# First pass of a two-layer transformer trunk: tables on other queues, one transfer per weight chunk, tokens in four parts, bias added behind the sums, one cast for both token blocks

## The chip, the cores and the metric

The kernel runs on 1 core of one Trainium2 chip. The metric is device time in microseconds. The kernel before took 645.62 us, the median of three runs (642.17 to 645.78).

The engines are named as the profile names them: PE does matmuls (PEld its weight loads), DVE is the vector engine, ACT the scalar engine, POOL the general one, SP issues most transfers.

## The reference

Two layers work on 256 tokens of width 1024. Layer 0 mixes tokens with block attention (one block of 256 here, so plain causal attention with 16 heads), layer 1 with differential attention; each is followed by a squared-ReLU MLP of width 4096. Each sub-layer's input is modulated by a vector c, and its output goes through a gate, a residual and a LayerNorm.

```
mod = jnp.einsum('bd,lde->lbe', jax.nn.silu(c), ada_w) + ada_b[:, None, :]
for i in range(DEPTH):
    shift1, scale1, gate1, shift2, scale2, gate2 = [m[:, None, :] for m in jnp.split(mod[i], 6, axis=-1)]
    h = x * (1.0 + scale1) + shift1
    y = moba_attention(h, ...)  # layer 0; layer 1: diff_attention(h, ...)
    x = layer_norm(DEEPNORM_ALPHA * x + (1.0 + gate1) * y, ln_g[i, 0], ln_b[i, 0])
    h = x * (1.0 + scale2) + shift2
    y = sq_relu_mlp(h, mlp_w_up[i], mlp_w_down[i])
    x = layer_norm(DEEPNORM_ALPHA * x + (1.0 + gate2) * y, ln_g[i, 1], ln_b[i, 1])
```

So before the first projection of layer 0 can start, silu(c), the two rows of `mod` for shift1 and scale1, and h must be there. `ada_w` reaches the kernel transposed, so that 128 outputs of `mod` are 128 partitions and the 1024 inputs lie along the row.

## The kernel before

All matmuls with weights are done in three products of rounded halves: a value is split into `hi` (a rounding cast on ACT) and `lo` (the difference, on DVE), and hi·hi + hi·lo + lo·hi are added in PSUM (`mm3`, lines L167 to L169). So each weight chunk that comes in as `raw` costs a cast on ACT (L130) and a subtraction on DVE (L131).

The **first pass** (`first_operand`, `first_products`) computes a first part of layer 0's q, k and v: columns 0 to 511 of each, for both token blocks of 128. It runs over the 8 chunks j of the contraction, 128 inputs each, and adds into six PSUM tiles (`kacc`: tags mm, sc, ac, for two blocks). For one chunk j it needs:

- two row sums for the modulation (`ada_rows`, L215 and L216): a 512 KB transfer of `ada_w` each into `aw`, then one DVE instruction that multiplies with silu(c) (`sbc`, spread over all partitions) and adds along the row, with the bias `ada_b` as the sum's start. They give the columns of `ab`, scale and shift; L499 adds 1 to the scale.
- the tokens: `xt` is transposed by PE into `tp` (L516), ACT forms `full` = tp·scale + shift (L518), then per block a cast to hi (L521) and a subtraction to lo (L522), both into `hT`.
- the weights: three transfers into one `raw` tile (L508 for v, L510 twice for q and k), then two casts and two subtractions, of 1024 and of 512 columns.
- 18 matmuls of 512 columns: 2 blocks, 3 outputs, 3 products.

The bias columns come from `tabT`, the transpose of a table `t1` (ada_b in 96 rows, ln_g in 32), which SP fetches ahead of the first `aw`; so does the identity `ident` that PE needs for all its transposes.

What is in which place on an engine is settled when the kernel is built: a scheduler orders each engine's instructions by its own estimate, and each engine then works through its list in order. Transfers are ordered the same way on the queue of the engine that issues them; SP's are tracked by eight semaphores in turn, so that an issue waits for the landing of the one eight places before. Buffers: `aw` tiles 2 and 3 (two tags), `raw` 3, `hi` and `lo` 8 each.

After the first pass the program string of layer 0 goes on with attention (V, Q, T, S, P, F steps), output projection, LayerNorm and MLP. Row sums for the other modulation vectors are done as fillers between.

Of the kernel before, what the change touches and what calls it, by code (L numbers as in the profile page):

```python
# [66 lines left out]
SHIFT1, SCALE1, GATE1, SHIFT2, SCALE2, GATE2 = range(6)  # L67
C_ID, C_ONE, C_MASK, C_ROPE = 0, 128, 256, 512
# [4 lines left out]
def tile_trunk(ctx: ExitStack, tc: tile.TileContext, x, c, moba_w_in, moba_w_out, diff_w_in, diff_w_out,  # L73
               lam_q1, lam_k1, lam_q2, lam_k2, subln_g, ada_wt, ada_b, ln_g, ln_b, w_up, w_down, cst, out):
    nc = tc.nc
    vec, act, pe, pool_e, sp = nc.vector, nc.scalar, nc.tensor, nc.gpsimd, nc.sync
# [5 lines left out]
    small = ctx.enter_context(tc.tile_pool(name="small", bufs=1))  # L82
# [10 lines left out]
    ident, ones = cs[:, C_ID:C_ID + P], cs[:, C_ONE:C_ONE + P]  # L93
    sbc = cpool.tile([P, D], F32, name="sbc")
    t1 = ap_.tile([P, P], F32, tag="nat", name="t1", bufs=3)
    t2 = ap_.tile([P, P], F32, tag="nat", name="t2", bufs=3)
    ccol = small.tile([P, 2, KC], F32, tag="ccol", name="ccol", bufs=1)
    sp.dma_start(out=ccol[:, 0, :], in_=c.rearrange("o (p k) -> p (o k)", k=KC))
    sp.dma_start(out=ident, in_=cst[:, C_ID:C_ID + P])
    sp.dma_start(out=t1[0:96, :], in_=ada_b.rearrange("l (j p) -> (l j) p", p=P))  # L100

    nhalf = small.tile([P, 1], F32, name="nhalf")
    pool_e.memset(nhalf, -0.5)

    act.activation(out=ccol[:, 1, :], in_=ccol[:, 0, :], func=AF.Exp, scale=-1.0)
    vec.tensor_scalar(out=ccol[:, 1, :], in0=ccol[:, 1, :], scalar1=1.0, scalar2=None, op0=ALU.add)
    vec.reciprocal(out=ccol[:, 1, :], in_=ccol[:, 1, :])
    vec.tensor_tensor(out=ccol[:, 1, :], in0=ccol[:, 1, :], in1=ccol[:, 0, :], op=ALU.mult)
# [15 lines left out]
        xt.append(xb)  # L124


    def split_piece(raw_ap, n=1024):
        hi = wp.tile([P, 1024], F32R, tag="hi", name="hi", bufs=8)
        lo = wp.tile([P, 1024], F32R, tag="lo", name="lo", bufs=8)
        act.copy(out=hi[:, :n], in_=raw_ap)  # L130
        vec.tensor_tensor(out=lo[:, :n], in0=raw_ap, in1=hi[:, :n], op=ALU.subtract)  # L131
        return hi, lo

    def raw_tile():
# [53 lines left out]
    cols = {}  # L188
    tabT = cpool.tile([P, P], F32, name="tabT")
    tabT2 = cpool.tile([P, P], F32, name="tabT2")  # L190

    def adab_cols(l, v):
        o = (l * 6 + v) * KC
        return tabT[:, o:o + KC]
# [13 lines left out]
            if filler:  # L208
                filler.popleft()()

    def ada_rows(l, v, j, dst, tag, bufs):

        aw = ap_.tile([P, D], F32, tag=tag, name="aw", bufs=bufs)
        r0 = v * D + j * P
        sp.dma_start(out=aw, in_=ada_wt[l, r0:r0 + P, :])  # L215
        vec.tensor_tensor_reduce(out=aw, in0=aw, in1=sbc, scale=1.0, scalar=adab_cols(l, v)[:, j:j + 1],  # L216
                                 op0=ALU.mult, op1=ALU.add, accum_out=dst)

    def queue_vector(l, v):
# [270 lines left out]
    hT0 = act_tiles()  # L490
# [3 lines left out]
    def first_operand(j):  # L494

        ab = small.tile([P, 2], F32, tag="ab0", name="ab0", bufs=3)
        ada_rows(0, SCALE1, j, ab[:, 0:1], "bc", 3)
        ada_rows(0, SHIFT1, j, ab[:, 1:2], "aw", 2)
        vec.tensor_scalar(out=ab[:, 0:1], in0=ab[:, 0:1], scalar1=1.0, scalar2=None, op0=ALU.add)  # L499
        def load_x(cols):  # L500
            for b in range(2):
                sp.dma_start(out=xt[b][:, cols], in_=x[0, b * P:(b + 1) * P, cols])

        if j == 0:
            load_x(slice(0, 256))
# [40 lines left out]
    tps = psum("tp")  # L546
# [16 lines left out]
    tps = psum("tp")  # L563
# [223 lines left out]
```

## Time and profile before

| | |
|---|---|
| median of three runs | 645.62 us |
| time of the profiled execution | 644.11 us |
| its span | 640.7 us |
| PE busy in the span | 609.0 us, 95% |
| DVE busy | 500.4 us, 78% |
| ACT busy | 377.6 us, 59% |
| POOL busy | 22.2 us, 3% |
| matmuls | 3140 |

The span is what the trace covers; 3.4 us of the execution's own time lie around it. An engine is busy when an instruction other than a wait or an issue runs on it. PE is busy for nearly the whole span except at its start and end, so a change in the first 55 us moves the end as far as it moves PE's work after them.

### The profile page before, as it was taken

The numbers are of one execution on the slowest core, as the hardware profiler recorded it, in microseconds if no ns is written. First come the engines' busy times: TensorE is split into PE (matmuls) and PEld (weight loads), VectorE is DVE, ScalarE is ACT, GpSimd is POOL, SyncE is SP. The second block draws the span as 40 slices with busy tenths as digits, with TensorE's granted clock in tenths as the row PEclk, the third lists the DMA queues.
The fourth block names the chain that finished last, engine by engine and source line by source line (L and its number), as shares of the span: only waits on it lengthen the run. The fifth ranks groups of instructions, "written<-read, shape, count | busy, mean of one in ns | idle before, by whom it ended". The sixth has DMA issues, their size and how long they took to land.

```text
span 640.7 us, 8768 instructions
## 1 busy us (share of the span) xinstructions
PE 609.0 (95%) x3140; PEld 499.6 (78%) x3140; DVE 500.4 (78%) x903; ACT 377.6 (59%) x699; POOL 22.2 (3%) x37
## 2 busy tenths in 40 slices
PE   4889999998999999999999999989999999999994
PEld 3667887886888888888877787767788888888883
DVE  5798998889978878888799989977984646465446
ACT  3448665657846545664477676765775556475530
POOL 0000000001000000000000010021100000000002
PEclk9999999999999999999999999999999999999998
DMA  8997998876689888989765967682663764746401
GB/s 292 406 322 279 313 325 286 288 250 227 215 309 343 308 313 330 326 294 338 268 231 188 337 229 263 232 289 68 208 218 109 259 225 143 255 133 213 182 0 66
DMA packets 65941, 158.23 MB, mean 247 GB/s; under 512 B 4041, under 2 KB 21098, under 8 KB 65898
## 3 DMA queue, kind: packets, MB, share of 16 engines
q1 hardware_dynamic: 65898, 157.68, 70.1%
q8 instruction: 24, 0.39, 0.2%
q14 instruction: 19, 0.16, 0.1%
HBM read 156.62 MB, written 1.05 MB: 246 GB/s over the span
## 4 chain that ended last, share of the span: by engine, by line
PE 64%; DVE 18%; DMA 6%; ACT 4%; issue 3%; POOL 2%; SPq 1%; DVEq 0%; POOLq 0%; ACTq 0%
PE ac L184 13%; PE sc L184 10%; PE mm L687 7%; PE tp L687 6%; DMA aw<-in_ada_w_dram 6%; DVE lo L131 5%; DVE aw L216 4%; PE mm L167 4%; PE mm L169 4%; PE mm L168 4%; PE mm L692 3%; PE tp L692 3%; ACT hi L130 2%; DVE z L292 1%; DVE z L289 1%
## 5 line engine op out<-in xcount | busy, mean ns | idle before, releaser
L131 DVE TENSOR_TENSOR lo<-raw,hi 128x1024 fp32r<-128x1024 f32 x196 | 232.0, 1197 | 44.1 <-ACT hi L130 40.4
L130 ACT CAST hi<-raw 128x1024 fp32r<-128x1024 f32 x196 | 201.3, 1034 | 62.5 <-PE sc L184 43.6
L216 DVE CUSTOM_DVE_ANT_0 aw<-aw,sbc,tabT 128x1024 f32<-128x1024 f32 x96 | 122.0, 1280 | 23.1 <-DMA aw<-in_ada_w_dram 22.7
L167 PE MATMUL mm<-hi,hT 128*128 128x512 f32 x224 | 90.6, 405 | 6.1 <-ACT hi L130 3.2
L169 PE MATMUL mm<-hi,hT 128*128 128x512 f32 x224 | 89.0, 398 | 0.0
L168 PE MATMUL mm<-lo,hT 128*128 128x512 f32 x224 | 88.6, 396 | 0.2 <-DVE lo L131 0.2
L687 PE MATMUL mm<-hT,hi 128*128 128x512 f32 x192 | 60.4, 396 | 0.0
L687 PE MATMUL tp<-hT,hi 128*128 128x512 f32 x192 | 60.3, 395 | 0.0
L167 PEld LDWEIGHTS mm<-hi,hT 128*128 128x128 f32 x224 | 42.3, 189 | 16.1 <-ACT hi L130 3.8
L184 PE MATMUL ac<-hi,sTh 128*128 128x512 f32 x160 | 51.2, 397 | 0.0
L184 PE MATMUL ac<-lo,sTh 128*128 128x512 f32 x160 | 50.8, 394 | 0.0
L184 PE MATMUL ac<-hi,sTl 128*128 128x512 f32 x160 | 50.4, 392 | 0.0
L169 PEld LDWEIGHTS mm<-hi,hT 128*128 128x128 f32 x224 | 42.3, 189 | 9.1 <-DVE hT L328 0.4
L168 PEld LDWEIGHTS mm<-lo,hT 128*128 128x128 f32 x224 | 42.3, 189 | 8.6 <-DVE lo L131 0.3
L184 PE MATMUL sc<-hi,sTh 128*128 128x512 f32 x144 | 45.3, 392 | 0.0
L184 PE MATMUL sc<-lo,sTh 128*128 128x512 f32 x144 | 45.1, 391 | 0.0
L184 PE MATMUL sc<-hi,sTl 128*128 128x512 f32 x144 | 44.6, 390 | 0.0
L692 PEld LDWEIGHTS tp<-hT,lo 128*128 128x128 f32 x192 | 34.4, 188 | 7.5
L692 PEld LDWEIGHTS mm<-hT,lo 128*128 128x128 f32 x192 | 34.4, 188 | 7.3
L697 ACT COPY nat<-mm 128x256 f32<-128x256 f32 x24 | 7.8, 376 | 52.4 <-PE mm L687 52.4
L692 PE MATMUL tp<-hT,lo 128*128 128x256 f32 x192 | 36.0, 279 | 0.0
L692 PE MATMUL mm<-hT,lo 128*128 128x256 f32 x192 | 35.9, 279 | 0.0
(153 smaller groups left out, 899.4 us busy)
## 6 DMA issues: line engine op xcount, KB each, us to landing
aw<-in_ada_w_dram SPq DMA_DIRECT2D x96, 512.0 KB, 5.5
raw<-in_mlp_w_up_dram SPq DMA_DIRECT2D x32, 1024.0 KB, 5.9
raw<-in_mlp_w_down_dram SPq DMA_DIRECT2D x32, 1024.0 KB, 5.1
raw<-in_diff_w_in_dram SPq DMA_DIRECT2D x16, 512.0 KB, 5.1
raw<-in_moba_w_in_dram SPq DMA_DIRECT2D x24, 256.0 KB, 5.5
raw<-in_moba_w_in_dram SPq DMA_DIRECT2D x8, 512.0 KB, 4.8
raw<-in_moba_w_out_dram SPq DMA_DIRECT2D x4, 1024.0 KB, 8.4
raw<-in_diff_w_in_dram SPq DMA_DIRECT2D x4, 1024.0 KB, 5.7
```

The source lines that it names most:

```text
L130: act.copy(out=hi[:, :n], in_=raw_ap)
L131: vec.tensor_tensor(out=lo[:, :n], in0=raw_ap, in1=hi[:, :n], op=ALU.subtract)
L167: pe.matmul(dst, lhsT=xh, rhs=wh, start=start, stop=False)
L168: pe.matmul(dst, lhsT=xh, rhs=wl, start=False, stop=False)
L169: pe.matmul(dst, lhsT=xl, rhs=wh, start=False, stop=stop)
L184: pe.matmul(dsts[h], lhsT=a, rhs=w[:, h * 512:(h + 1) * 512], start=start and k == 0 and i == 0, stop=stop and k == n - 1 and i == 2)
L216: vec.tensor_tensor_reduce(out=aw, in0=aw, in1=sbc, scale=1.0, scalar=adab_cols(l, v)[:, j:j + 1], op0=ALU.mult, op1=ALU.add, accum_out=dst)
L289: vec.tensor_tensor(out=z[:, c_], in0=accs[c_.start // 512][:, a0:a0 + c_.stop - c_.start], in1=gate[:, c_], op=ALU.mult)
L292: vec.scalar_tensor_tensor(out=z[:, c_], in0=xt[b][:, c_], scalar=ALPHA, in1=z[:, c_], op0=ALU.mult, op1=ALU.add)
L687: pe.matmul(ps, lhsT=w[k][0][:, c_], rhs=x3[k], start=first, stop=last)
L692: pe.matmul(ps[:, 0:S], lhsT=w[k][1][:, c_], rhs=x3[k][:, 0:S], start=False, stop=False)
L697: act.copy(out=r[:, i * S:(i + 1) * S], in_=ps[:, S:2 * S])
```

## The change

In words: `ident` is issued from ACT's queue, and the two parts of `t1` from POOL's, so SP issues the first `aw` right behind c. A chunk's weights come in one transfer of three pieces of 512 columns, q and k first in the tile, v last. The tokens come in four pairs of transfers of 256 columns (chunks 0, 2, 4, 6) in place of one pair of 256 columns and one of 768. The row sums start from 0; the biases (1 added to those of scale) lie in a new tile `tab1`, and one addition on two columns (L505 of the changed file) adds them behind the sums, shift first. `full` is cast to hi for both blocks by one ACT instruction and made into lo by one DVE instruction. Weight casts are written with v's 512 columns ahead of q's and k's 1024. `tabT` is copied by ACT in place of DVE. Three instructions (the exponential of c, the copy into `tab1`, the subtractions of chunk 0) are kept in the order of the program text.

```diff
-    sp.dma_start(out=ident, in_=cst[:, C_ID:C_ID + P])
-    sp.dma_start(out=t1[0:96, :], in_=ada_b.rearrange("l (j p) -> (l j) p", p=P))
+    act.dma_start(out=ident, in_=cst[:, C_ID:C_ID + P])
+    pool_e.dma_start(out=t1[0:96, :], in_=ada_b.rearrange("l (j p) -> (l j) p", p=P))
+    pool_e.dma_start(out=t1[96:128, :], in_=ln_g.rearrange("l i (j p) -> (l i j) p", p=P))
...
-    act.activation(out=ccol[:, 1, :], in_=ccol[:, 0, :], func=AF.Exp, scale=-1.0)
+    tc.keep_in_program_order(act.activation(out=ccol[:, 1, :], in_=ccol[:, 0, :], func=AF.Exp, scale=-1.0))
...
-    def ada_rows(l, v, j, dst, tag, bufs):
+    def ada_rows(l, v, j, dst, tag, bufs, bias=True):
...
-        vec.tensor_tensor_reduce(out=aw, in0=aw, in1=sbc, scale=1.0, scalar=adab_cols(l, v)[:, j:j + 1],
+        vec.tensor_tensor_reduce(out=aw, in0=aw, in1=sbc, scale=1.0, scalar=adab_cols(l, v)[:, j:j + 1] if bias else 0.0,
...
-        ada_rows(0, SCALE1, j, ab[:, 0:1], "bc", 3)
-        ada_rows(0, SHIFT1, j, ab[:, 1:2], "aw", 2)
-        vec.tensor_scalar(out=ab[:, 0:1], in0=ab[:, 0:1], scalar1=1.0, scalar2=None, op0=ALU.add)
+        ada_rows(0, SHIFT1, j, ab[:, 0:1], "bc", 3, False)
+        ada_rows(0, SCALE1, j, ab[:, 1:2], "aw", 2, False)
+        if j == 0:
+            tc.keep_in_program_order(vec.tensor_copy(out=tab1[:, 0:KC], in_=adab_cols(0, SHIFT1)))
+            vec.tensor_scalar(out=tab1[:, KC:], in0=adab_cols(0, SCALE1), scalar1=1.0, scalar2=None, op0=ALU.add)
+        vec.tensor_tensor(out=ab, in0=ab, in1=tab1[:, j:j + KC + 1:KC], op=ALU.add)
+        if j % 2 == 0:
             for b in range(2):
+                cols = slice(j * P, (j + 2) * P)
                 sp.dma_start(out=xt[b][:, cols], in_=x[0, b * P:(b + 1) * P, cols])
...
-        sp.dma_start(out=raw[:, 0:512], in_=wr[:, 2 * D:2 * D + 512])
-        for s_ in range(2):
-            sp.dma_start(out=raw[:, 512:1536].rearrange("p (g s n) -> p s g n", g=2, s=2)[:, s_],
-                         in_=wr[:, s_ * D:s_ * D + 512].rearrange("p (g n) -> p g n", n=256))
-        if j == 1:
-            load_x(slice(256, D))
+        sp.dma_start(out=raw[:, 0:1536].rearrange("p (s n) -> p s n", s=3),
+                     in_=wr.rearrange("p (s d) -> p s d", s=3)[:, :, 0:512])
...
-        act.activation(out=full[:, :256], in_=tp[:, :256], func=AF.Identity, scale=ab[:, 0:1], bias=ab[:, 1:2])
-        for b in range(2):
-            hi, lo = halves(hT0[j // 4], b)
-            act.copy(out=hi[:, j % 4, :], in_=full[:, b * P:(b + 1) * P])
-            vec.tensor_tensor(out=lo[:, j % 4, :], in0=full[:, b * P:(b + 1) * P], in1=hi[:, j % 4, :], op=ALU.subtract)
-        h1, l1 = split_piece(raw[:, 0:1024])
-        h2, l2 = split_piece(raw[:, 1024:1536], 512)
-        return [(h1[:, 0:512], l1[:, 0:512]), (h1[:, 512:1024], l1[:, 512:1024]), (h2[:, 0:512], l2[:, 0:512])]
+        act.activation(out=full[:, :256], in_=tp[:, :256], func=AF.Identity, scale=ab[:, 1:2], bias=ab[:, 0:1])
+        both = hT0[j // 4][:, j % 4, :]
+        act.copy(out=both[:, 0:2 * P], in_=full[:, :2 * P])
+        vec.tensor_tensor(out=both[:, 2 * P:], in0=full[:, :2 * P], in1=both[:, 0:2 * P], op=ALU.subtract)
+        v_w = [t[:, 0:512] for t in split_piece(raw[:, 1024:1536], 512, j == 0)]
+        qk_w = [t.rearrange("p (s n) -> p s n", s=2) for t in split_piece(raw[:, 0:1024], keep=j == 0)]
+        return [v_w] + [[t[:, :, g * 256:(g + 1) * 256] for t in qk_w] for g in range(2)]
...
-    vec.tensor_copy(out=tabT, in_=tps[:, 0:P])
+    act.copy(out=tabT, in_=tps[:, 0:P])
```

Since the scheduler orders the instructions anew, the change also moves work in the lists. On SP, the start of the program before; c is the conditioning vector, cs the constants with the identity, t the table, aw the rows of `ada_w`, raw the weights:

```order
L98 DMA ccol<-in_c_dram 128x8
L99 DMA cs<-in_constants_dram 128x128
L100 DMA t_73<-in_ada_b_dram 96x128
L533 DMA t_73<-in_ln_g_dram 32x128
L215 DMA aw<-in_ada_w_dram 128x1024 x2
L502 DMA x<-in_x_dram 128x256 x2
L508 DMA raw<-in_moba_w_in_dram 128x512
L510 DMA raw<-in_moba_w_in_dram 128x2x256 x2
```

and in the changed kernel:

```order
L98 DMA ccol<-in_c_dram 128x8
L218 DMA aw<-in_ada_w_dram 128x1024 x2
L509 DMA x<-in_x_dram 128x256 x2
L512 DMA raw<-in_moba_w_in_dram 128x3x512
```

Three issues ahead of the first `aw` are gone, and two of the three for `raw`.

On ACT, chunks 4 and 5 of the first pass before (raw_295 and full_302 belong to chunk 4, raw_342 and full_349 to chunk 5):

```order
L130 CAST hi_308<-raw_295 128x1024
L518 ACTIVATE full_302<-tp_299,ab0_287 128x256
L130 CAST hi_312<-raw_295 128x512
L521 CAST hT_102<-full_302 128x128 x2
L130 CAST hi_355<-raw_342 128x1024
L518 ACTIVATE full_349<-tp_346,ab0_334 128x256
L130 CAST hi_359<-raw_342 128x512
L521 CAST hT_102<-full_349 128x128 x2
```

and now (raw_284 and full_289 belong to chunk 4, raw_327 and full_332 to chunk 5):

```order
L518 ACTIVATE full_289<-tp_286,ab0_274 128x256
L520 CAST hT_103<-full_289 128x256
L131 CAST hi_293<-raw_284 128x512
L131 CAST hi_297<-raw_284 128x1024
L518 ACTIVATE full_332<-tp_329,ab0_319 128x256
L131 CAST hi_336<-raw_327 128x512
L520 CAST hT_103<-full_332 128x256
L131 CAST hi_340<-raw_327 128x1024
```

Before, the 1024-column cast of a chunk's weights stood ahead of that chunk's `full`; now both weight casts stand behind it. The chunks alternate between the two patterns shown: 2, 4 and 6 as chunk 4, and 3, 5 and 7 as chunk 5.

On DVE, chunk 4 before, from its row sums on:

```order
L216 ISA aw_288,ab0_287<-aw_288,sbc_72,tabT_99 128x1024
L216 ISA aw_291,ab0_287<-aw_291,sbc_72,tabT_99 128x1024
L499 TENSOR_SCALAR ab0_287<-ab0_287 128x1
L131 TENSOR_TENSOR lo_309<-raw_295,hi_308 128x1024
L131 TENSOR_TENSOR lo_313<-raw_295,hi_312 128x512
L522 TENSOR_TENSOR hT_102<-full_302,hT_102 128x128 x2
```

and now the end of chunk 3, chunk 4 and the start of chunk 5 (lo_253 belongs to chunk 3, ab0_319 to chunk 5):

```order
L219 ISA aw_275,ab0_274<-aw_275,sbc_72 128x1024
L132 TENSOR_TENSOR lo_253<-raw_239,hi_252 128x1024
L219 ISA aw_278,ab0_274<-aw_278,sbc_72 128x1024
L505 TENSOR_TENSOR ab0_274<-ab0_274,tab1_113 128x2
L521 TENSOR_TENSOR hT_103<-full_289,hT_103 128x256
L132 TENSOR_TENSOR lo_294<-raw_284,hi_293 128x512
L132 TENSOR_TENSOR lo_298<-raw_284,hi_297 128x1024
L219 ISA aw_320,ab0_319<-aw_320,sbc_72 128x1024
L219 ISA aw_323,ab0_319<-aw_323,sbc_72 128x1024
L505 TENSOR_TENSOR ab0_319<-ab0_319,tab1_113 128x2
```

In both, the subtractions stand behind the row sums and their addition; only in chunks 3, 5 and 7 does the first row sum of the next chunk now stand between the two subtractions. (Between two row sums the lists also hold the reading of the accumulator, left out here.)

## Rows read from the trace of the kernel before

**Rows 1.** Busy time in stretches (us, busy of each engine, clock, DMA share, GB/s).

```profile
12.00:30.00 18.00, 15.84 (x63) 12.18 (x64) 14.31 (x26) 7.29 (x16) 0.00 (x0) 1.00 1.05 402
30.00:50.00 20.00, 18.15 (x78) 13.57 (x76) 19.72 (x38) 10.28 (x21) 0.00 (x0) 1.00 0.93 340
55.00:100.00 45.00, 43.97 (x275) 35.23 (x273) 42.04 (x108) 32.76 (x77) 0.00 (x0) 1.00 0.85 289
100.00:160.00 60.00, 56.12 (x321) 45.42 (x321) 52.24 (x109) 36.12 (x79) 3.30 (x4) 1.00 0.76 260
```

**Rows 2.** Timeline of the start (start us, duration, engine, line, what, idle before and releaser).

```profile
0.72 1.28 ACT L105 ACT_TABLE_LOAD   x1 [0.72 <-PEq L771]
...
1.17 0.42 SPq L99 DMA_DIRECT2D cs<-in_constants_dram  x1
...
2.37 0.21 ACT L105 ACTIVATE ccol<-ccol 128x8 f32<-128x8 f32 x1 [0.37 <-DMA ccol<-in_c_dram]
2.57 0.90 SPq L215 DMA_DIRECT2D aw<-in_ada_w_dram  x2
2.61 0.17 DVE L106 TENSOR_SCALAR ccol<-ccol 128x8 f32<-128x8 f32 x1 [2.61 <-ACT ccol L105]
...
6.18 1.28 DVE L216 CUSTOM_DVE_ANT_0 aw<-aw,sbc,tabT 128x1024 f32<-128x1024 f32 x1 [0.24 <-DMA aw<-in_ada_w_dram]
...
8.76 0.15 DVE L499 TENSOR_SCALAR ab<-ab 128x1 f32<-128x1 f32 x1
...
10.70 1.56 ACT L130 CAST hi<-raw 128x1024 fp32r<-128x1024 f32 x2 [0.31 <-DMA raw<-in_moba_w_in_dram]
```

**Rows 3.** DMA issues of 0 to 60 us: KB each, median us to landing.

```profile
aw<-in_ada_w_dram SPq DMA_DIRECT2D x18, 512.0 KB, 8.0
...
cs<-in_constants_dram SPq DMA_DIRECT2D x1, 64.0 KB, 2.1
```

**Rows 4.** Timeline of ACT, chunk 3, and the first cast of chunk 4.

```profile
27.93 0.56 ACT L518 ACTIVATE full<-tp,ab 128x256 f32<-128x256 f32 x1 [3.91 <-DVE ab L499]
28.39 1.03 ACT L130 CAST hi<-raw 128x1024 fp32r<-128x1024 f32 x1
29.32 0.50 ACT L521 CAST hT<-full 128x128 fp32r<-128x128 f32 x2
29.72 0.62 ACT L130 CAST hi<-raw 128x512 fp32r<-128x512 f32 x1
31.00 1.05 ACT L130 CAST hi<-raw 128x1024 fp32r<-128x1024 f32 x1 [0.65 <-DMA raw<-in_moba_w_in_dram]
```

**Rows 5.** Timeline of DVE, chunk 3 to the end of chunk 4's row sums.

```profile
27.68 0.15 DVE L499 TENSOR_SCALAR ab<-ab 128x1 f32<-128x1 f32 x1
29.45 1.23 DVE L131 TENSOR_TENSOR lo<-raw,hi 128x1024 fp32r<-128x1024 f32 x1 [1.62 <-ACT hi L130]
30.60 0.49 DVE L522 TENSOR_TENSOR hT<-full,hT 128x128 fp32r<-128x128 f32 x2
31.00 0.68 DVE L131 TENSOR_TENSOR lo<-raw,hi 128x512 fp32r<-128x512 f32 x1
31.61 1.28 DVE L216 CUSTOM_DVE_ANT_0 aw<-aw,sbc,tabT 128x1024 f32<-128x1024 f32 x1
...
34.02 0.15 DVE L499 TENSOR_SCALAR ab<-ab 128x1 f32<-128x1 f32 x1
```

**Rows 6.** Timeline of DVE, the additions of chunks 6 and 7.

```profile
43.56 0.15 DVE L499 TENSOR_SCALAR ab<-ab 128x1 f32<-128x1 f32 x1
...
48.33 0.15 DVE L499 TENSOR_SCALAR ab<-ab 128x1 f32<-128x1 f32 x1
```

**Rows 7.** Timeline of PE: chunk 7's first and last matmul, and the next transposes.

```profile
49.90 0.50 PE L167 MATMUL mm<-hi,hT 128*128 128x512 f32 x1 [0.21 <-ACT hT L521]
...
53.90 0.39 PE L169 MATMUL ac<-hi,hT 128*128 128x512 f32 x1
...
55.59 0.63 PE L366 MATMUL tp<-cs,nat 128*128 128x128 f32 x4 [0.41 <-DVE nat L359]
```

More of the change, by code (lines that the diff above doesn't have):

```diff
@@ L124, in tile_trunk, with split_piece @@
         xt.append(xb)
-    def split_piece(raw_ap, n=1024):
+    def split_piece(raw_ap, n=1024, keep=False):
         hi = wp.tile([P, 1024], F32R, tag="hi", name="hi", bufs=8)
@@ L130, in split_piece @@
         act.copy(out=hi[:, :n], in_=raw_ap)
-        vec.tensor_tensor(out=lo[:, :n], in0=raw_ap, in1=hi[:, :n], op=ALU.subtract)
+        sub = vec.tensor_tensor(out=lo[:, :n], in0=raw_ap, in1=hi[:, :n], op=ALU.subtract)
+        if keep:
+            tc.keep_in_program_order(sub)
         return hi, lo
@@ L496, in first_operand @@
         ab = small.tile([P, 2], F32, tag="ab0", name="ab0", bufs=3)
-        ada_rows(0, SCALE1, j, ab[:, 0:1], "bc", 3)
-        ada_rows(0, SHIFT1, j, ab[:, 1:2], "aw", 2)
-        vec.tensor_scalar(out=ab[:, 0:1], in0=ab[:, 0:1], scalar1=1.0, scalar2=None, op0=ALU.add)
-        def load_x(cols):
+        ada_rows(0, SHIFT1, j, ab[:, 0:1], "bc", 3, False)
[5 more added lines that the diff above has]
+        if j % 2 == 0:
             for b in range(2):
+                cols = slice(j * P, (j + 2) * P)
                 sp.dma_start(out=xt[b][:, cols], in_=x[0, b * P:(b + 1) * P, cols])
-        if j == 0:
-            load_x(slice(0, 256))
         raw = raw_tile()
         wr = moba_w_in[0][j * P:(j + 1) * P, :]
-        sp.dma_start(out=raw[:, 0:512], in_=wr[:, 2 * D:2 * D + 512])
-        for s_ in range(2):
-            sp.dma_start(out=raw[:, 512:1536].rearrange("p (g s n) -> p s g n", g=2, s=2)[:, s_],
-                         in_=wr[:, s_ * D:s_ * D + 512].rearrange("p (g n) -> p g n", n=256))
-        if j == 1:
-            load_x(slice(256, D))
+        sp.dma_start(out=raw[:, 0:1536].rearrange("p (s n) -> p s n", s=3),
+                     in_=wr.rearrange("p (s d) -> p s d", s=3)[:, :, 0:512])
         tp = psum("tp")
@@ L531, in first_products @@
                 mm3(kacc[b][s_], (hi[:, j % 4, :], lo[:, j % 4, :]), ws[s_], j == 0, j == KC - 1)
-    sp.dma_start(out=t1[96:128, :], in_=ln_g.rearrange("l i (j p) -> (l i j) p", p=P))
     tps = psum("tp")
     pe.transpose(out=tps[:, 0:P], in_=t1, identity=ident)
-    vec.tensor_copy(out=tabT, in_=tps[:, 0:P])
+    act.copy(out=tabT, in_=tps[:, 0:P])
+    tab1 = small.tile([P, 2 * KC], F32, name="tab1")
     ws = first_operand(0)
```

## The prediction

> **What bounds the kernel now.** I read the busy table first: PE is busy 95% of the span, so a change in the first pass counts as far as PE's later work starts earlier or later. Then the stretches [rows 1]: from 12 to 30 us PE is busy 15.84 of 18 us with the transfers full (share 1.05, 402 GB/s), and from 30 to 50 us DVE is the full engine, 19.72 of 20. So two things share the pass, transfers at first and DVE from 30 us on. Then the timelines of DVE and ACT, chunk by chunk. In chunk 3 the addition L499 starts at 27.68, and DVE idles 1.62 us before the next subtraction [rows 5], because ACT's list has `full` first and only then the weight cast (27.93, 28.39) [rows 4]; the next addition comes at 34.02, 6.34 us after the last. From chunk 4 on ACT has done the 1024-column cast (31.00) ahead of `full` [rows 4]; DVE can subtract while ACT makes `full`, the idle time is gone, and the last two additions stand 4.77 us apart, 43.56 and 48.33 [rows 6]. That interval is all DVE work. From chunk 7's addition (48.33 + 0.15 = 48.48) PE needs 5.8 us: its first matmul of the chunk is at 49.90, the last ends at 53.90 + 0.39 = 54.29 [rows 7].
>
> **The start.** Three issues leave SP's queue ahead of the first `aw`: it goes from 2.57 to 1.17, 1.40 us earlier [rows 2]. That does not start the sums 1.40 earlier, since they need `sbc` too, and c's way to it is as before; the wait for `aw` that this removes is at most the 0.24 us before 6.18 [rows 2]. On ACT the issue of `ident` stands ahead of the table load: 0.72 + 0.42 (SP's issue) + 1.28 = 2.42, where the exponential started at 2.37; it loses 0.05. `ident` itself took 2.1 us to land [rows 3] and would be there at about 2.8, ahead of PE's first transposes. Two copies into `tab1` and the addition (0.15 each, as L499) end chunk 0's addition at about 8.9, as before (8.76 + 0.15) [rows 2].
>
> `t1` now comes through POOL, which no row before shows. PE's transpose of it, and ACT's copy behind that, stand ahead of the weight casts. From below it takes the 2.1 us of the table-sized transfer, from above the 8.0 us median of an `aw` in a full queue [rows 3]: landing between 2.8 and 8.7. The casts wait for weights until about 9.2 (below), so even the upper end costs 0.2 us at most; I take 0, since the rows are small transfers before the queue is full.
>
> A rule speaks against this part. The Trainium skill (DMA: Bandwidth & Descriptors, Rules for kernel authors) says that spreading transfers over SP, ACT and GpSimd gives no bandwidth and saves issue time only. The trace agrees as to where the gain must end: the 1.40 us are issue time. By that rule this part is worth at most 1.40 us; by my walk it is worth what the next steps leave of it.
>
> **Chunks 0 to 2.** Weights of chunk 0 were complete just before 10.70 [rows 2]; 1.40 earlier, with a little for two issues less, is about 9.2. ACT's list now has both weight casts, then `full`: 9.25, then 0.5 and 0.95 from start to start, so `full` starts at 10.7 and hT's hi ends at about 11.7. DVE has filled the time with the first sum of chunk 1. It subtracts hT (0.33, a 256-wide one taken between half of the pair's 0.49 and the 0.68 of the 512-wide one [rows 5]), 512 columns (0.6), 1024 (1.15), then the second sum, and the addition ends at 15.3. In chunk 1 both casts stand ahead of `full`, no idle time: + 4.77, so chunk 2's addition ends at 20.1. The old kernel had its chunk 3 addition end at 27.83.
>
> **Chunks 2 to 7: the main term.** Here both casts stand behind `full`. From an addition's end, with ACT starting 0.09 later, `full` 0.56, casts of 0.39 (256 wide, estimated between 0.25 and 0.62), 0.62 and 1.04 [rows 4]:
> - chunks 2, 4, 6 (full, hT, v, qk): hT's lo can start at 1.16, lo of v at 1.66, lo of q and k at 2.60; two sums of 1.20 each and the addition's 0.29 behind the second (0.08 for the accumulator, 0.06, 0.15) end at about 6.4. DVE idles 1.6 us in it. The row nearest to it, chunk 3 before, has 1.62 us idle and 6.34 [rows 5].
> - chunks 3, 5, 7 (full, v, hT, qk): lo of v at 1.23, hT's lo at 1.83, a sum at 2.17, lo of q and k at 3.4 without a wait, a sum, the addition: 6.0.
>
> So additions end at 8.9, 15.3, 20.1, 26.5, 32.5, 38.9, 44.9 and 51.4. Before, the last three intervals had no idle time. At chunk 4 the change is ahead (32.5 against 34.02 + 0.15 = 34.17), at chunk 6 it is 1.2 behind (44.9 against 43.71), at chunk 7 2.9 behind (51.4 against 48.48). The saving on hT (one instruction less on each of ACT and DVE, some 0.1 us a chunk) is in these sums. Behind the addition PE needs the same 5.8 us: cast of v, cast of hT, 18 matmuls. **Main term: + 2.9 us** at the end of the pass. Its ends: with no idle time at all from chunk 2 on, 20.1 + 5 x 4.77 = 43.9, that is - 4.6; with 6.4 in every chunk 52.1, + 3.6. I take the walk, since rows 5 have its pattern.
>
> Transfers do not set this pace: a chunk needs 1.05 MB of `ada_w`, 0.79 of weights and 0.13 of tokens on average, 4.9 us at 402 GB/s [rows 1], less than 6.2. The tokens in four parts move 0.79 MB, 2.0 us at that rate, from the first two chunks into later ones with room. POOL, ACT and SP queues have nothing else behind the moved issues.
>
> **Behind the pass.** Before, the last chunk finished block 0's q and k first, and PE then waited 0.41 us in the transposes [rows 7]. Now both blocks finish together: block 0's q and k are complete six matmuls (1.4 us) before the end, then a copy, the rotary steps on DVE, transposes, a copy by ACT, and the scores right behind. I put the added wait at 0.6 us. Then the lists of attention are in another order up to the MLP of layer 0, and the same from there. PE was idle 1.03 us from 55 to 100 and 3.88 from 100 to 160 [rows 1]; that is the most a better order could give, and I take as much for a worse one. Value taken: 0.
>
> **Sum.** 2.9 + 0.6 = + 3.5 us. The profiled execution took 644.11 us, so 647.6; the median of the runs is 1.51 above that execution, which gives **649** us, 0.5% more. One per cent (6.5 us) is about what a measurement of this kernel tells from no change.
>
> **Rivals.**
> 1. *Faster: transfers were the true limit and casts keep ahead.* For it: a DMA share above 1 until 30 us. The pass would end 1.40 earlier from the issues and about 0.4 from larger pieces: 643.8; with no idle time on DVE at all, - 4.6: 641.0. Against it: chunk 3's idle time ended on ACT, not on a transfer [rows 5]. Chance 0.17.
> 2. *Absorbed.* The 3.5 us fall into PE's 4.9 us of later idle time [rows 1], as transfers and fillers that made it are issued by engines that are not late: about 646. Against it: DVE is busy 42.04 of 45 us from 55 to 100. Chance 0.18.
> 3. *Slower, worse order in attention.* PE waits up to 4.9 us more between 55 and 160: up to 654. Chance 0.13.
> 4. *Slower, tables late.* POOL's transfers land after 8.6 us, and PE's transpose, ACT's casts and the rest wait, one for one: with a landing at 11.6, 652. Against it: the rows of all table-sized transfers. Chance 0.07. The Trainium skill (SBUF — State Buffer, SBUF: two separate sides) says that POOL cannot write descriptors while DVE runs certain copies. DVE is idle until 2.61 and then has three short instructions [rows 2]; by that rule nothing is late here.
>
> My forecast has the remaining 0.45.
>
> **How the numbers follow.** The likeliest case gives 649. The range takes in rivals 1 and 2 from 642.5 and most of 3, up to 653; about a tenth is left out on each side. Below 639.2 (faster by over 1%) needs rival 1 at its best and attention's idle time besides: 0.03. Above 652.1 lie most of rival 3 and of rival 4: 0.13. Within 1%: 0.84.
>
> **What would show it.** Right: DVE idle 1.2 to 1.6 us behind each addition of chunks 2 to 7, ended by ACT's casts; additions some 6.2 us apart on average; chunk 4 ahead of before and chunk 7 behind; the first `aw` issued at 1.2; the pass's last matmul ending near 57. Wrong: intervals of 4.8 with casts waiting for transfers (rival 1); PE's transpose of `t1` or ACT's copy of it as the last wait before the first casts (rival 4); the pass late but the layer's MLP on time (rival 2), or PE idle for more than 5 us between the pass and the MLP (rival 3).

## The result: 0.9% slower, 649.39 us, and the profile after

The changed kernel took 649.39 us (median of 7 runs), the kernel before 643.92 us (median of 7). The ratio is 1.0089, with a 95% interval of 1.0063 to 1.0115: slower by 5.7 us, less than the 1% that I called no change. One run of the changed kernel, 658.74 us at a granted clock of 0.984, counts as a slow one and is left out of the ratio. The profiled execution took 649.46 us (before 644.11), its span 647.5 us (before 640.7).

The same stretches as [rows 1], after the change (us, busy of PE, PEld, DVE, ACT and POOL, granted clock, DMA share, GB/s):

```profile
12.00:30.00 18.00, 16.74 (x67) 13.19 (x68) 15.18 (x29) 7.29 (x13) 0.00 (x0) 1.00 1.04 412
30.00:50.00 20.00, 16.73 (x70) 11.88 (x69) 15.74 (x26) 7.21 (x12) 0.00 (x0) 1.00 0.89 309
55.00:100.00 45.00, 42.64 (x253) 33.65 (x252) 39.31 (x109) 28.47 (x69) 0.00 (x0) 1.00 0.73 251
100.00:160.00 60.00, 55.66 (x329) 45.04 (x328) 53.01 (x115) 36.27 (x82) 1.65 (x2) 1.00 0.77 271
```

Until 30 us PE does more than before. From 30 to 50 us DVE, which had been full (19.72 of 20), is busy 15.74 us, and PE's busy time falls by 1.42 us. From 55 to 100 us it falls by another 1.33.

The start, from the timeline of the changed kernel (start us, duration, engine, line, what, idle before and what ended it), beside [rows 2]:

```profile
1.17 0.92 SPq L218 DMA_DIRECT2D aw<-in_ada_w_dram  x2
...
2.84 0.21 ACT L106 ACTIVATE ccol<-ccol 128x8 f32<-128x8 f32 x1 [0.41 <-DMA ccol<-in_c_dram]
...
6.37 1.23 DVE L219 CUSTOM_DVE_ANT_0 aw<-aw,sbc 128x1024 f32<-128x1024 f32 x1 [2.68 <-ACT sbc L118]
7.21 0.45 PE L533 MATMUL tp<-cs,t 128*128 128x128 f32 x1 [1.49 <-DMA t<-in_ln_g_dram]
...
8.94 0.16 DVE L505 TENSOR_TENSOR ab<-ab,tab 128x2 f32<-128x2 f32 x1
...
9.61 1.56 ACT L131 CAST hi<-raw 128x512 fp32r<-128x512 f32 x2 [1.66 <-DMA raw<-in_moba_w_in_dram]
```

Its small transfers (KB each, median us from issue to landing), and last the transfer of c in the kernel before:

```profile
t<-in_ada_b_dram POOLq DMA_DIRECT2D x1, 48.0 KB, 4.4
ccol<-in_c_dram SPq DMA_DIRECT2D x1, 4.0 KB, 2.1
t<-in_ln_g_dram POOLq DMA_DIRECT2D x1, 16.0 KB, 5.1
```

```profile
ccol<-in_c_dram SPq DMA_DIRECT2D x1, 4.0 KB, 1.6
```

The first `aw` is issued at 1.17 us, and the tables come from POOL in time: PE transposes them at 7.21, and the casts at 9.61 wait for weights.

DVE in chunks 6 and 7, where [rows 6] had two additions 4.77 us apart:

```profile
44.37 0.16 DVE L505 TENSOR_TENSOR ab<-ab,tab 128x2 f32<-128x2 f32 x1
45.66 0.43 DVE L521 TENSOR_TENSOR hT<-full,hT 128x256 fp32r<-128x256 f32 x1 [1.13 <-ACT hT L520]
...
47.12 1.22 DVE L132 TENSOR_TENSOR lo<-raw,hi 128x1024 fp32r<-128x1024 f32 x1 [0.26 <-ACT hi L131]
...
50.67 0.16 DVE L505 TENSOR_TENSOR ab<-ab,tab 128x2 f32<-128x2 f32 x1
52.03 0.69 DVE L132 TENSOR_TENSOR lo<-raw,hi 128x512 fp32r<-128x512 f32 x1 [1.20 <-ACT hi L131]
```

Behind the addition of each of the chunks 2 to 7 DVE is idle 1.2 to 1.4 us in all (in chunk 6, 1.13 and 0.26), ended by ACT's casts, and the interval from chunk 6 to 7 is 6.30 us. The eight additions end at 9.10, 15.61, 20.18, 26.53, 32.37, 38.68, 44.53 and 50.83 us.

PE at the end of the pass, beside [rows 7]:

```profile
52.36 0.73 PE L170 MATMUL mm<-hi,hT 128*128 128x512 f32 x2 [1.51 <-ACT hT L520]
...
56.37 0.40 PE L172 MATMUL ac<-hi,hT 128*128 128x512 f32 x1
...
58.56 0.78 PE L420 MATMUL sc<-qkT 64*128 64x128 f32 x8 [0.68 <-ACT qkT L371]
...
61.33 0.66 PE L369 MATMUL tp<-cs,nat 128*128 128x128 f32 x4 [0.49 <-ACT qkT L371]
```

The pass ends at 56.77 us, 2.48 later than before (54.29). Both traces have 3140 matmul records, so the same matmul can be found in both by counting from the end. It comes 5.77 us later from 160 to 320 us (layer 0's MLP). So 2.48 us arose in the pass and 3.3 us between the pass and the MLP. PE's idle time grew there too. The windows from the end of the pass to the MLP's first matmul, before and after, leave 4.44 and 6.70 us of it:

```profile
54.29:148.40 94.11, 89.67 (x547) 72.56 (x547) 83.98 (x205) 60.81 (x140) 1.65 (x2) 1.00 0.82 282
```

```profile
56.77:154.39 97.62, 90.92 (x548) 73.10 (x548) 85.89 (x208) 60.52 (x143) 1.65 (x2) 1.00 0.77 268
```

Behind 320 us single traces are a poor guide. In the LayerNorm between the layers PE waits 0.42 us in the kernel before and 3.57 us in experiment 12, which has the same lists there; so traces are compared up to the MLP.

### The profile page after: what moved, and what is told of

Its sections match the earlier page's. It is cut to its first block, busy times and chain, and to the rows that moved or that the text cites. A ratio compares the mean times of both kernels' runs of the same rounds, so it can differ in the third digit from the quotient of the medians.

```text
span 647.5 us, 8734 instructions
## 1 busy us (share of the span) xinstructions
PE 610.8 (94%) x3140; PEld 499.5 (77%) x3140; DVE 498.7 (77%) x896; ACT 375.3 (58%) x692; POOL 23.4 (4%) x39
## 4 chain that ended last, share of the span: by engine, by line
PE 39%; DVE 19%; DMA 9%; issue 4%; ACT 3%; POOL 2%; POOLq 0%; DVEq 0%; SPq 0%; ACTq 0%
DMA aw<-in_ada_w_dram 9%; PE ac L187 8%; DVE lo L132 6%; PE sc L187 6%; DVE aw L219 4%; PE tp L687 4%; PE mm L687 4%; PE mm L172 3%; PE mm L170 3%; PE mm L171 3%; PE tp L692 2%; PE mm L692 2%; ACT hi L131 1%; DVE z L295 1%; DVE z L292 1%
## 5 line engine op out<-in xcount | busy, mean ns | idle before, releaser
L132 DVE TENSOR_TENSOR lo<-raw,hi 128x1024 fp32r<-128x1024 f32 (+1 forms) x196 | 231.7, 1196 | 43.2 <-ACT hi L131 40.2
L131 ACT CAST hi<-raw 128x1024 fp32r<-128x1024 f32 (+1 forms) x196 | 200.3, 1035 | 55.0 <-PE sc L187 33.1
L219 DVE CUSTOM_DVE_ANT_0 aw<-aw,sbc,tabT 128x1024 f32<-128x1024 f32 x80 | 102.1, 1280 | 32.4 <-DMA aw<-in_ada_w_dram 32.2
L187 PEld LDWEIGHTS ac<-lo,sTh 128*128 128x128 f32 x160 | 30.0, 188 | 8.7 <-DVE lo L132 2.8
```

What stands on the lines that cost most here:

```text
L132: sub = vec.tensor_tensor(out=lo[:, :n], in0=raw_ap, in1=hi[:, :n], op=ALU.subtract)
L187: pe.matmul(dsts[h], lhsT=a, rhs=w[:, h * 512:(h + 1) * 512], start=start and k == 0 and i == 0, stop=stop and k == n - 1 and i == 2)
```

## The experiments

A scheduler orders the instructions, so an edit in the pass also reorders attention far behind it. To part the two, the experiments (none has the number 8) hold every engine's list behind the pass fixed, and most of them the pass's as well, by a list of instruction numbers taken from one of the kernels (this and the edits below are shortened):

```diff
+    for offsets in order.values():
+        for a, b in zip(offsets, offsets[1:]):
+            tc.add_manual_dep(made[b], made[a].name, <no semaphore>, reason="pin")
```

This adds no wait between engines. "Order of before" and "order of the changed kernel" mean the lists behind the pass.

### 1 and 5: the changed pass with the order of before

Experiment 1: the changed kernel's text with

```diff
+    pin(REST_OF_BEFORE)
```

> The changed first pass, with everything behind it held in the order that it had before the change, on every engine. Theory A (the end of the first pass, 2.5 us later, is handed on and the order behind the pass costs the rest): 2.5 to 3.3 us slower than before, so a ratio of 1.004 to 1.005. Theory B (the lateness of the pass alone makes everything, the order behind it nothing): the same +5.5 to +6 as the changed kernel, ratio about 1.009. Theory C (only the order behind the pass matters, the later end of the pass is absorbed): within 1 us of before.

Measured: 649.93 us, ratio 1.0100 (1.0067 to 1.0133). That looks like theory B (the lateness of the pass alone makes everything), but the trace shows a fault of the experiment. DVE's timeline has

```profile
57.93 0.19 DVE L666 COPY tabT<-tp 128x33 f32<-128x33 f32 x1 [2.41 <-PE tp L665]
```

A small PE transposition (33 rows of constants) was ahead of chunk 7's products in the kernel before; here it came behind all 18, and DVE's list, with the rotation of q and k behind that copy, stood still. Experiment 5 holds the pass's own order too and puts the transposition back:

```diff
-    pass, T(33 rows), attention
+    pass up to chunk 6, T(33 rows), products of chunk 7, attention
```

> The first experiment again, with one TensorE instruction moved: the transposition of the 33 rows of the attention's constants stands ahead of chunk 7's products, as in the kernel before; in the first experiment it came behind them (57.65 us), VectorE waited 2.41 us for it and TensorE 1.90 us for VectorE. Theory A (the pass's end hands on 2.5 us, and the order behind the pass costs the rest of the changed kernel's +5.5): about 2 us less than the first experiment, 646.5 to 648 us, ratio 1.003 to 1.006. Theory B (the lateness of the pass makes all of it, whatever the order behind): the same as the first experiment, ratio 1.009 to 1.010.

Measured: 646.72 us, ratio 1.0054 (1.0032 to 1.0076), as theory A has it. One misplaced transposition had cost some 3 us: 0.46% between the ratios, and 3.47 us in the MLP of the two traces. (The pairs 3 and 6, 4 and 11 below give 0.27 and 0.16%; each of the three is uncertain by some 0.4%.) In experiment 5 the pass's last matmul is

```profile
56.59 0.40 PE L298 MATMUL ac<-hi,hT 128*128 128x512 f32 x1
```

so the pass ends at 56.99 us, 2.70 later than before, and the MLP starts 2.21 later: in this trace most of the pass's lateness is handed on.

The two experiments also show how far one trace can be trusted. Their lists on PE, ACT and DVE in the pass up to chunk 7's addition are those of the changed kernel, and the transfers are the same; yet that addition ends at 51.83 and 51.04 us, and at 50.83 in the changed kernel. Experiment 1's delay arises in chunk 2, whose `full` waits there for PE's transposition of the tokens, not for the addition. A difference of less than 1 us between single traces of this pass shows nothing. (The kernel before is steadier: 48.48 us, and 48.43 and 48.45 in experiments 2 and 9.)

### 2: only the order behind the pass

The text of the kernel before with

```diff
+    pin(REST_OF_CHANGED)
```

> The first pass of the kernel before, unchanged, with everything behind it in the order of the changed kernel. Theory A: about +3 us (what is left of the +5.5 when the pass ends as before), ratio about 1.005. Theory B: within 1 us of before. Theory C: the whole +5.5 to +6 us, ratio about 1.009.

Measured: 647.65 us, ratio 1.0061 (1.0037 to 1.0085). The pass ends at 54.23, as before; the loss is all behind it. PE's timeline:

```profile
109.96 0.50 PE L302 MATMUL ac<-lo,sTh 128*128 128x512 f32 x1 [2.38 <-DVE lo L249]
...
124.39 0.63 PE L484 MATMUL tp<-cs,nat 128*128 128x128 f32 x4 [2.06 <-DVE nat L477]
```

And what DVE did ahead of that `lo`:

```profile
105.42 1.28 DVE L334 CUSTOM_DVE_ANT_0 aw<-aw,sbc,tabT 128x1024 f32<-128x1024 f32 x1
...
107.03 1.27 DVE L334 CUSTOM_DVE_ANT_0 aw<-aw,sbc,tabT 128x1024 f32<-128x1024 f32 x1
...
108.69 1.21 DVE L249 TENSOR_TENSOR lo<-raw,hi 128x1024 fp32r<-128x1024 f32 x1
```

The scheduler has put two filler sums ahead of the subtraction that PE waits for. The changed kernel has the same wait in the same place (2.37 us at 111.86); the kernel before has none there. The second wait, 2.06 us, is only 0.50 in the changed kernel. With experiment 5 all four corners are there: the new order costs 0.61% with the pass of before and 0.35% with the changed one (1.0089 against 1.0054); the changed pass costs 0.54% in the order of before and 0.28% in the new one. 0.61 and 0.54 are ratios to the kernel before, uncertain by some 0.25%, so each of the two is a loss by itself. 0.35 and 0.28 are differences of two ratios, uncertain by some 0.35%: they don't tell whether the two add up. The traces say it in the MLP of layer 0: later by 2.21 us with the changed pass alone, 4.55 with the new order alone, 5.77 with both.

### 3 and 6: the casts ahead of `full`

The changed pass, chunks 2 to 7, in the order of before behind it:

```diff
-    ACT: full, hT hi, v hi, qk hi        (odd chunks: full, v, hT, qk)
-    DVE: sums, addition, hT lo, v lo, qk lo
+    ACT: v hi, qk hi, full, hT hi
+    DVE: sums, addition, v lo, qk lo, hT lo
```

> The changed first pass with one thing moved: in chunks 2 to 7 ScalarE casts both parts of the weights ahead of full, and VectorE subtracts the weights behind the addition and the tokens last; behind the pass the order of before, as in the first experiment. If VectorE's idle time of 1.2 us a chunk behind ScalarE's casts sets the pace of the pass, the additions come 4.8 us apart instead of 6.1, the pass ends 4 to 6.5 us earlier than in the first experiment and before that of the kernel before too, and the time is 641 to 645 us. The rival, that transfers set the pace (1.97 MB a chunk at the 355 to 412 GB/s that the rows show is 4.8 to 5.5 us, and the moved issues delay them), lets the pass gain less than 1.5 us against the first experiment.

Measured: 642.84 us, ratio 0.9993 (0.9968 to 1.0018), inside its range. It has the fault of experiment 1: the pass ends at 51.07 us and PE then waits 1.90 us. Experiment 6 has the transposition in its place:

> The third experiment (weights cast ahead of full in chunks 2 to 7) with the same transposition ahead of chunk 7's products. If VectorE's waits behind ScalarE's casts set the pace of the pass and its end is handed on, the gap of 2.4 us behind the pass closes and the time is 639 to 641.5 us, ratio 0.992 to 0.996, faster than either kernel. The rival, that the work behind the pass waits for its transfers whatever the pass does, leaves 642 to 644 us, ratio 0.998 to 1.001.

Measured: 640.83 us, ratio 0.9966 (0.9939 to 0.9993): the time is inside its range, the ratio just above it. It is faster than both kernels and 0.9% faster than experiment 5, from which it differs by the places of those instructions alone. The pass's last matmul,

```profile
50.45 0.39 PE L298 MATMUL ac<-hi,hT 128*128 128x512 f32 x1
```

ends at 50.84 us, 6.15 earlier than in experiment 5. ACT's timeline shows the next limit:

```profile
34.36 1.57 ACT L257 CAST hi<-raw 128x512 fp32r<-128x512 f32 x2 [2.94 <-DMA raw<-in_moba_w_in_dram]
...
39.43 1.57 ACT L257 CAST hi<-raw 128x512 fp32r<-128x512 f32 x2 [2.60 <-DMA raw<-in_moba_w_in_dram]
```

The casts now wait for the weights' landing. The additions come 4.63, 4.56, 5.13, 5.40 and 5.07 us apart (chunks 2 to 7): in the last three DVE is idle 0.25 to 0.67 us each for casts that waited for weights, most in the fourth:

```profile
35.02 0.69 DVE L258 TENSOR_TENSOR lo<-raw,hi 128x512 fp32r<-128x512 f32 x1 [0.41 <-ACT hi L257]
35.97 1.23 DVE L258 TENSOR_TENSOR lo<-raw,hi 128x1024 fp32r<-128x1024 f32 x1 [0.26 <-ACT hi L257]
```

### 4 and 11: the casts behind `full` in the kernel before

```diff
     chunks 4 to 7
-    ACT: qk hi, full, v hi, hT hi, hT hi
-    DVE: sums, L499, qk lo, v lo, hT lo, hT lo
+    ACT: full, qk hi, hT hi, hT hi, v hi
+    DVE: sums, L499, qk lo, hT lo, hT lo, v lo
```

> The kernel before with one thing moved: in chunks 4 to 7 ScalarE casts the weights behind full, as chunk 3 has it, and VectorE subtracts them there; transfers, tables, tokens and the order behind the pass as before. If the casts behind full set the pace, four chunks lose 1.2 to 1.6 us each: the pass ends 4 to 6 us later and the time is 3 to 6 us longer, ratio 1.005 to 1.009. The rival, that transfers and the moved issues cost the time, leaves it within 1 us of before.

> The fourth experiment again (the kernel before with the casts of chunks 4 to 7 behind full), with the transposition of the 33 rows ahead of chunk 7's products as in the kernel before. If VectorE's waits for ScalarE's casts set the pace, what is left of the +7.4 us of the fourth experiment is its later additions (4.5 us at chunk 7) and a part behind them: 647 to 650 us, ratio 1.006 to 1.010. If transfers set the pace, it is within 1 us of before.

Measured: 651.60 us, ratio 1.0131 (1.0096 to 1.0167), and with the transposition in its place 650.30 us, 1.0115 (1.0090 to 1.0140). In experiment 11 nothing in the kernel before was changed but this order, and it costs about as much as the whole change (1.0089; the intervals overlap). DVE waits 1.63 us behind each addition of the chunks 3 to 7 for a cast, here chunk 6's,

```profile
48.58 1.23 DVE L258 TENSOR_TENSOR lo<-raw,hi 128x1024 fp32r<-128x1024 f32 x1 [1.63 <-ACT hi L257]
```

and chunk 7's addition ends at 53.29, 4.81 later than before. That is as expected; both times are above their ranges (experiment 4's by more, with the fault of experiment 1), and the windows of experiment 11 show a part of why:

```profile
46.00:48.00 2.00, 1.67 (x8) 1.05 (x6) 0.95 (x3) 0.95 (x2) 0.00 (x0) 1.00 0.35 110
48.00:50.00 2.00, 0.63 (x2) 0.33 (x3) 1.42 (x3) 1.47 (x4) 0.00 (x0) 1.00 0.70 233
50.00:52.00 2.00, 2.00 (x6) 1.59 (x7) 2.00 (x6) 0.00 (x0) 0.00 (x0) 0.55 0.78 292
52.00:54.00 2.00, 2.00 (x7) 1.59 (x6) 1.29 (x5) 0.62 (x2) 0.00 (x0) 0.59 0.86 260
54.00:56.00 2.00, 2.00 (x9) 1.29 (x8) 1.08 (x1) 1.81 (x4) 0.00 (x0) 1.00 1.06 422
```

PE was busy 0.63 of the 2 us from 48 to 50, and then the granted clock was 0.55 and 0.59, mostly the level of 1.2 GHz; matmuls started 0.43 us apart in place of 0.23. So chunk 6's products ran late into chunk 7's. The pass ends at 60.37, 6.08 later than before, of which 1.3 came behind the addition.

### 7, 12 and 13: the tables and the transfers

Experiment 7, the changed kernel in its own order:

```diff
-    act.dma_start(out=ident, ...);  pool_e.dma_start(out=t1[0:96, :], ...);  pool_e.dma_start(out=t1[96:128, :], ...)
+    sp.dma_start(out=ident, ...);   sp.dma_start(out=t1[0:96, :], ...);      sp.dma_start(out=t1[96:128, :], ...)
```

> The changed kernel with the constants and both tables issued from SP again, ahead of the first transfer for the sums; every other engine in the changed kernel's order throughout. If VectorE's waits set the pace, the start's 0 to 1.5 us are absorbed or handed on and the time is within 1.5 us of the changed kernel, ratio 1.006 to 1.011. The rival, that the moved issues cost the changed kernel its time (c landed at 2.1 us instead of 1.6 and ln_g 5.1 us behind its issue), gives 3 us or more back, ratio below 1.005.

Measured: 651.46 us, ratio 1.0140 (1.0108 to 1.0173), so slower than the changed kernel by 0.5% (uncertain by some 0.4%): a little outside what was expected, and away from the rival. The first `aw` is again issued at 2.57 us. Chunk 0's addition comes only 0.3 us later, but DVE then waits for the third `aw`:

```profile
11.76 1.22 DVE L345 CUSTOM_DVE_ANT_0 aw<-aw,sbc 128x1024 f32<-128x1024 f32 x1 [2.35 <-DMA aw<-in_ada_w_dram]
```

That sum started at 10.91 in the changed kernel. From chunk 1 on the additions are 0.9 to 1.25 us later than in the changed kernel; chunk 7's, at 52.08, is 0.25 and 1.04 later than in experiments 1 and 5, which have the same pass and the queues of the change. So the queues give 0.2 to 1.25 us at the end of the pass. The Trainium skill (DMA: Bandwidth & Descriptors, Rules for kernel authors) says that other queues save issue time only, and this stays within the 1.40 us of issue time that they saved. In the MLP the trace is 1.48 us behind the changed kernel's, with a PE wait of 3.35 us in attention in place of 2.37. What makes the rest of the 0.5% is open.

Experiment 12, the kernel before with the queues alone:

```diff
-    sp.dma_start(out=ident, ...);   sp.dma_start(out=t1[0:96, :], ...);      sp.dma_start(out=t1[96:128, :], ...)
+    act.dma_start(out=ident, ...);  pool_e.dma_start(out=t1[0:96, :], ...);  pool_e.dma_start(out=t1[96:128, :], ...)
```

> The kernel before with the constants issued from ScalarE's queue and both tables from GpSimd's, nothing else changed, every other engine in its order of before. VectorE copies the tables ahead of its sums there, so if ln_g lands at about 7 us the first sum starts at about 7.7 instead of 6.18, while the transfers behind the first come 1 us earlier, as the seventh experiment lets expect; the two leave chunk 1 and later between 1 us earlier and 0.5 us later, and the time within 1.5 us of before, ratio 0.997 to 1.002. If the tables' queues were worth the 2 to 3 us that the seventh experiment shows, ratio 0.995 to 0.997.

Measured: 643.42 us, ratio 1.0008 (0.9987 to 1.0029). DVE's timeline:

```profile
8.24 0.29 DVE L663 COPY tabT<-tp 128x128 f32<-128x128 f32 x1 [4.75 <-PE tp L662]
8.67 1.28 DVE L343 CUSTOM_DVE_ANT_0 aw<-aw,sbc,tabT 128x1024 f32<-128x1024 f32 x1
```

Here the sums need the tables, so they wait for POOL's transfers: the first starts at 8.67 in place of 6.18, and chunk 7's addition ends 1.26 us later. The queues gained nothing here; they gained only where the addition stands behind the sums. The trace shows one more thing: PE is 1.23 us late at 100 us, 0.18 at 110, and in the MLP it is 0.62 us ahead. So with the order of before a lateness of this size was absorbed whole, where experiment 5's was handed on for the most part.

Experiment 13, the changed kernel in its own order:

```diff
-    sp.dma_start(out=raw[:, 0:1536] as three pieces, ...)
+    for s_ in range(3):
+        sp.dma_start(out=raw[:, s_ * 512:(s_ + 1) * 512], in_=wr[:, s_ * D:s_ * D + 512])
     tokens: columns 0 to 255 ahead of chunk 0's weights, 256 to 1023 behind chunk 1's
```

> The changed kernel with its weights in three transfers a chunk again and the tokens in two parts as before (columns 0 to 255 ahead of the weights of chunk 0, the rest behind those of chunk 1); tables, sums, casts and every other engine's order as in the changed kernel. If the transfers are hidden behind VectorE's pace, within 1.5 us of the changed kernel, ratio 1.006 to 1.012. If single transfers delay what the pass waits for, it gives back 2 us or more, ratio below 1.005; if they gain, ratio above 1.013.

Measured: 651.44 us, ratio 1.0143 (1.0113 to 1.0172). In the trace chunk 7's addition ends at 51.36, 0.53 us later than in the changed kernel; DVE's waits behind ACT are the same 1.13 and 1.20. That lies inside the spread of the same pass in experiments 1 and 5, so a worth of the larger transfers is not shown. Of the 0.5% between the medians I can't say what made it, and the two intervals just touch. In the profiled run 0.52 us is still there in the MLP; behind it PE waits 2.36 us between the layers in place of 0.97, and the granted clock there is 0.57 and 0.58 (334 to 338 us), where the changed kernel's is 1.00.

### 9 and 10: the order behind the pass once more

Experiment 9, the kernel before, with VectorE's and ScalarE's lists behind the pass from the changed kernel, SP's and TensorE's from before:

> The kernel before, with only VectorE's and ScalarE's order behind the pass taken from the changed kernel; SP's and TensorE's order there as before. If the second experiment's +3.9 us are made by VectorE's order (two sums of 1.21 us each put ahead of rotation and of the subtraction that TensorE waits for, 2.38 us), it is 3 to 5 us slower than before, ratio 1.005 to 1.008. If SP's order of transfers or TensorE's own order makes them, it is within 1.5 us of before.

Measured: 668.04 us, ratio 1.0407 (1.0364 to 1.0449). Neither theory expected that: it seems that lists from two schedules wait for each other. PE's timeline has, among others,

```profile
99.05 0.63 PE L484 MATMUL tp<-cs,nat 128*128 128x128 f32 x4 [2.76 <-DVE nat L477]
...
120.79 1.09 PE L484 MATMUL tp<-cs,nat 128*128 128x128 f32 x4 [5.93 <-DVE nat L477]
```

The experiment does not tell which engine's list is to blame. Experiment 10 puts the early pass of experiment 6 ahead of the changed kernel's whole order:

> The early pass of the third and sixth experiments (weights cast ahead of full in chunks 2 to 7) with everything behind it in the changed kernel's own order. If the pass and the order behind it cost separately, the early pass gives back about what it gave between the fifth and the sixth experiment (5.9 us) and the order keeps its price of 2 to 4 us: 643 to 646 us, ratio 1.000 to 1.004. If the order of the changed kernel costs only because its pass ends late, it is as fast as the sixth experiment, ratio 0.995 to 0.998.

Measured: 643.54 us, ratio 1.0007 (0.9986 to 1.0027). Its pass ends at 50.35 us, and still it is 0.41% slower than experiment 6 (uncertain by some 0.35%), and 5.1 us later in the MLP of the traces: the order costs by itself, however early the pass. PE waits at the same place, and here the clock fell behind it:

```profile
104.80 0.80 PE L313 MATMUL ac<-lo,sTh 128*128 128x512 f32 x1 [2.85 <-DVE lo L258]
```

```profile
104.00:106.00 2.00, 1.20 (x4) 1.05 (x5) 2.00 (x3) 0.00 (x0) 0.00 (x0) 0.70 0.87 287
106.00:108.00 2.00, 2.00 (x9) 1.44 (x7) 2.00 (x3) 0.86 (x2) 0.00 (x0) 0.50 0.80 248
108.00:110.00 2.00, 2.00 (x20) 1.79 (x20) 1.78 (x6) 0.37 (x1) 0.00 (x0) 0.94 0.92 332
```

Three more runs have this wait in this place. In experiment 13 it is as long as in the changed kernel, and the clock fell behind it:

```profile
112.19 0.62 PE L313 MATMUL ac<-lo,sTh 128*128 128x512 f32 x1 [2.37 <-DVE lo L258]
```

```profile
112.00:114.00 2.00, 1.81 (x8) 1.74 (x9) 2.00 (x4) 0.30 (x1) 0.00 (x0) 0.60 1.00 358
114.00:116.00 2.00, 2.00 (x13) 1.35 (x12) 2.00 (x4) 0.93 (x3) 0.00 (x0) 0.54 0.96 358
```

In experiment 7 it is longer than in all the others, and the clock stayed at 1.00, as it did in experiment 2 behind 2.38 us:

```profile
114.51 0.50 PE L313 MATMUL ac<-lo,sTh 128*128 128x512 f32 x1 [3.35 <-DVE lo L258]
```

So the length of the wait alone does not tell whether the clock falls.

## Why the prediction was right, and which term was not

- **The start.** Issue at 1.17 and tables before the casts came as predicted. c's landing did not: 2.1 us in place of 1.6, so the exponential started 0.47 later, not 0.05, and the first sum 0.19 later. Chunk 0's addition ended at 9.10 for 8.9, and the casts began at 9.61 for 9.25. The tables landed inside the bounds of 2.8 to 8.7, nearer the upper one than I had taken; as they cost nothing there, the sum did not suffer and rival 4, late tables, did not come true (experiment 12 shows what they cost where the sums wait for them).
- **Chunks 0 to 2.** 15.3 and 20.1 predicted, 15.61 and 20.18 measured. A wait is in it that the walk did not have: DVE stood 1.81 us for the third `aw`, until 10.91.
- **The main term.** Predicted additions at 26.5, 32.5, 38.9, 44.9 and 51.4, measured 26.53, 32.37, 38.68, 44.53 and 50.83; idle times of 1.2 to 1.6 predicted, 1.2 to 1.4 measured. The pass ends 2.48 us later for 2.9; the same pass in experiments 1 and 5 ends 3.42 and 2.70 later. That the order of the casts makes it is shown from both sides: experiments 3 and 6 take the waits away and the pass ends over 6 us earlier, experiments 4 and 11 bring them into the kernel before and it loses 1.2 to 1.3%.
- **Rival 1, transfers as the limit.** Wrong for this change, since DVE's waits in chunks 2 to 7 ended on ACT. But transfers stand close behind: with the casts ahead, intervals settle at 5.1 to 5.4 us and the casts wait for weights. My lower end of 4.77 us an interval (- 4.6 us) was too good: experiment 6, with the casts ahead, ends its pass 3.45 us ahead of before.
- **Rival 2, absorbed.** Wrong for this change: in experiment 5, 2.21 of 2.70 us were still there in the MLP. But not without grounds, as experiment 12 absorbed 1.23 us.
- **Behind the pass: the term that was mis-sized.** I had + 0.6 for waits at the first scores and 0 for the new order of attention, with bounds of 4.9 us. The bound came from PE's idle time before; that limits what a better order can give, but nothing limits a worse one to as much. Measured: 3.3 us together in the trace, 2.3 us (experiment 5 against the changed kernel) to 3.9 us (experiment 2) for the order in the medians, uncertain by 2.2 and 1.5 us. The first scores do wait 0.68 and the next transposes 0.49 us; the largest single wait is the 2.37 us at 111.86. So rival 3 came true together with the forecast and not instead of it, at a half to four fifths of its upper price. My sign for it came true as well, PE idle for more than 5 us between the pass and the MLP: 6.70 us, though 4.44 before makes that a weak sign. A part of the price in the medians may be the clock: the runs with the changed order (the changed kernel, experiments 2, 7, 10 and 13) have median granted clocks of 0.991 to 0.994, those of the kernel before and experiments 5, 6 and 12 0.995 to 0.996. But experiments 1, 3, 4 and 11 have the order of before and lie at 0.988 to 0.993, so a lower clock does not belong to this order alone. How much it costs I can't separate: in the profiled run of the changed kernel the clock stayed at 1.00 behind the wait, so the 3.3 us of the traces have nothing of it.
- **Sum.** + 3.5 us predicted, + 5.7 measured by the ratio, + 5.35 between the two profiled executions; 649 us predicted, 649.39 measured. That the medians agree more closely than the sums is luck: I started from a median of three (645.62), and that of seven was 1.7 us lower, which made up for most of the 2 us that the sum lacks.

## What to carry to other kernels

Where one engine rounds and a second subtracts, look at what the first has queued behind its wait for the second: a cast that needs only a transfer belongs ahead of the step that waits for the other engine, or the second idles once per chunk. A change that shortens issues, transfers and instruction counts can lose more by the order in which a scheduler then lists them; so hold the lists fixed to measure a part by itself, and look behind the changed stage for new waits of the full engine. And one small instruction that is placed behind a long row of others can hold up an engine that is not in that row: the transposition of 33 rows cost 1 to 3 us in three pairs of experiments.

## What the runs showed of the hardware

- c's 4 KB landed 2.1 us (the changed kernel) and 1.9 us (experiment 10) behind its issue when ACT's and POOL's queues issued at the same time, 1.6 us (the kernel before, experiment 2) when SP issued alone. Why is not shown.
- POOL's transfers of 48 and 16 KB landed 4.4 and 5.1 us behind their issue in the changed kernel, 5.1 and 5.6 in experiments 10 and 12. The same 16 KB from SP landed in 2.3 us in experiment 7.
- The granted clock fell to the level of 1.2 GHz behind PE waits of 2.85 us (experiment 10) and 2.37 us (experiment 13), and stayed at 2.4 GHz behind waits of 2.37 us (the changed kernel), 2.38 us (experiment 2) and 3.35 us (experiment 7) in the same place.
